# Expert weights by pairs of adjacent rows in a two-layer hybrid diffusion trunk

## The chip, the cores and the metric

The kernel runs on one core of one Trainium2 chip. The metric is the time of one execution on the device in microseconds (us). The kernel before took 2174.04, 2175.32 and 2178.39 us in three runs, median 2175.32. The profile is one execution, taken by the hardware profiler. Its engines are PE (matmul), PEld (PE's weight loads), DVE, ACT, POOL and SP; SP computes nothing and issues most of the transfers, a few are issued by ACT. Sixteen DMA engines carry all transfers.

## The reference

Two layers of one trunk run over 256 context tokens and 256 latent tokens of width 1024, all in fp32. Each layer first mixes tokens in three branches (an S5 state-space model, a Mamba-2 style SSD, windowed attention), merges them and adds the result to the stream x. Then follows the part that the change is about, a mixture of 16 experts of which each chooses its tokens. The context is routed as a set of its own, and it is not needed after layer 0, so layer 1 routes the latent tokens alone.

```python
def expert_choice_ffn(h, w_router, w_gate, w_up, w_down):
    cap = EC_CAPACITY_FACTOR * n // N_EXPERTS              # 2 * 256 / 16 = 32 tokens an expert
    aff = softmax(einsum('bnd,de->bne', h, w_router))
    g, idx = lax.top_k(swapaxes(aff, 1, 2), cap)
    xe = vmap(lambda hb, ib: hb[ib])(h, idx)                # (b, 16, 32, 1024)
    hid = silu(einsum('becd,edf->becf', xe, w_gate)) * einsum('becd,edf->becf', xe, w_up)
    ye = einsum('becf,efd->becd', hid, w_down) * g[..., None]
    # scatter-add of ye to the tokens

h2 = rmsnorm(x, norm2_g[i]) * (1.0 + sc2) + sh2             # sc2, sh2: from silu(c) @ w_mod[i] + b_mod[i]
x = x + g2 * expert_choice_ffn(h2, w_router[i], w_e_gate[i], w_e_up[i], w_e_down[i])
```

Each of the three matrices of an expert is 1024 x 1024 fp32, 4 MB; an expert has 12 MB, a layer's experts 192 MB (MB is 1,048,576 bytes where tiles are counted). In every product the sum runs over 1024 features (or 1024 hidden units), and a sum may take its terms in any order, so long as both factors use the same one.

## The kernel before, in words

**Stages.** Function `mixing` computes a layer's branches and, at its end, the router (`router_prep`, `router_half`, lines 1140 to 1200). Function `moe` (line 1239) picks the tokens (`top`, `pick`), gathers them, and goes through the 16 experts. After layer 1 a last norm writes the output. Modulation vectors (sh1, sc1, g1, sh2, sc2, g2, kinds 0 to 5) come from `mod_group` (line 159), which computes half of one vector in 32 small matmuls; these groups are filled in beside the mixing stage by `fill`. Kinds 3 and 4 are sh2 and sc2, which the experts' input uses.

**Features on partitions.** The contraction runs over partitions, so the 1024 features are cut into 8 blocks of 128. Before the change block k holds features 128k to 128k+127, partition p feature 128k + p. `gather` (line 1274) makes the transposed, selected tokens `xeT[:, k, e, :]` by a matmul of the token tile x (as weights, columns of block k) with a one-hot matrix; ScalarE or VectorE apply sc2 and sh2 per partition on the way out of PSUM. The expert's hidden units are transposed by four PE transposes (lines 1398 and 1428) into `hT`, again in blocks of 128.

**Loading the weights.** `wtiles` (line 1340) is a generator: it takes the next buffer, has SP load it, and yields the k blocks for the matmuls. A buffer of tag xw or rb8 holds 2048 columns a partition (1 MB, two blocks at full width), one of tag w, wh or wl 1024 columns (512 KB, one block). Which tag comes next is told by a list, `ring`: the first tag in it that is not larger than what is left of the matrix is taken and moved to the end. Layer 0 has 4 xw and 4 rb8, layer 1 has 6 xw and 4 rb8, both have 3 w, 2 wh and 2 wl. In layer 0 two xw buffers are lent to `s5_params`, which prepares layer 1's S5 constants during expert 4 (line 1377). The transfer itself is

```python
SP.dma_start(w, src[k0 * 128:(k0 + nk) * 128, c0:c0 + c].rearrange("(k p) c -> p k c", p=128))
```

so a partition of a large buffer receives row p of one block and row p of the next, 128 rows apart in memory: two runs of 4 KB. The down matrix of the last expert is loaded in two halves of 512 columns (`down`, line 1350), in runs of 2 KB, so that its first half can be finished early.

**Order of the work.** Gate and up take 32 matmuls an expert (line 1389 in layer 0, 1419 in layer 1), then come a tanh on ACT, two products on DVE, the transposes, and 16 matmuls of down (1405 and 1436). DVE scales the result into `YE` (1409, 1441); every four experts in layer 0 and every two in layer 1, `combine` (1363) scatters YE back to x by matmuls (1366) and adds it on DVE. Each engine's order is fixed when the program is built: a planner simulates the program and lets an instruction go ahead of others whose buffer isn't free yet in the simulation. On the chip each queue then runs strictly in that order. SP is one such queue: a transfer that waits for its buffer holds up all transfers behind it.

Of the kernel before, what the change touches and what calls it, by code (L numbers as in the profile page):

```python
# [61 lines left out]
def r(ap):  # L62
    return ap.bitcast(F32R)


@with_exitstack
def tile_trunk(ctx: ExitStack, tc: tile.TileContext, a, out, dbg=None, stop=None):
# [91 lines left out]
    def mod_group(l, kind, h):  # L159
        ps = bank("mm")  # L160
        for u in range(4):
            w = load_w(a["w_mod"][l], 2 * u, 2, kind * D + h * 512, 512, split=False)
            for i in range(2):
                for j in range(4):
                    PE.matmul(ps[32 * j:32 * j + 32, :128], sil[:, 2 * u + i, :], w[:, i, j * 128:j * 128 + 128],
                              start=u == 0 and i == 0, stop=u == 3 and i == 1)
# [296 lines left out]
    def mixing(l, mods):  # L463
# [673 lines left out]
        SP.dma_start(wr, a["w_router"][l].rearrange("(k p) e -> p k e", p=128))  # L1137
# [16 lines left out]
        def router_half(st, hf):  # L1154
            wrs, rbias = rts[st]
            xts = []
            for k2 in range(2):
                ps = bank("mm")
                for j in range(2):
                    k = 4 * hf + 2 * k2 + j  # L1160
                    for q in range(2):
                        PE.transpose(ps[:, j * 256 + q * 128:j * 256 + q * 128 + 128],
                                     x[:, 2 * st + q, k * 128:k * 128 + 128], ident)
# [75 lines left out]
    def moe(l, mods):  # L1239
# [34 lines left out]
        def gather(e0, e1, gs=sts):  # L1274
            w_ = (e1 - e0) * 32
            per = 1 if w_ * len(gs) > 512 else len(gs)
            for k in range(8):
                for s0 in range(0, len(gs), per):
                    ps = bank()
                    for si, st in enumerate(gs[s0:s0 + per]):  # L1280
                        for q in range(2):
                            tt = 2 * st + q
                            PE.matmul(ps[:, si * w_:si * w_ + w_], x[:, tt, k * 128:k * 128 + 128], oh[tt][:, e0:e1, :],  # L1283
                                      start=q == 0, stop=q == 1)
# [45 lines left out]
        def wtile(left, c):  # L1330
            tag = next(t for t in ring if (2048 if t in big else 1024) <= left * c)
# [8 lines left out]
        def wtiles(src, c0=0, c=D):  # L1340
            k0 = 0
            while k0 < 8:
                w = wtile(8 - k0, c)
                nk = w.shape[1]
                SP.dma_start(w, src[k0 * 128:(k0 + nk) * 128, c0:c0 + c].rearrange("(k p) c -> p k c", p=128))
# [29 lines left out]
        for e in range(16):  # L1375
# [8 lines left out]
            if full:  # L1384
# [12 lines left out]
                for j in range(4):  # L1397
                    PE.transpose(pt[:, j * 128:j * 128 + 128], hd[:, j * 128:j * 128 + 128], ident)
# [14 lines left out]
            else:  # L1413
# [13 lines left out]
                for j in range(4):  # L1427
                    PE.transpose(pt[:, j * 64:j * 64 + 64], hd[64:128, j * 128:j * 128 + 128], ident[64:128, 64:128])
# [75 lines left out]
def _layout(inp):  # L1504
# [8 lines left out]
    def s5cols(v):  # L1513
# [3 lines left out]

    s5d = _np.zeros((2, 8, 4, 32), g["s5_d"].dtype)
# [3 lines left out]
        "norm1": cols(g["norm1_g"]), "norm2": cols(g["norm2_g"]),  # L1522
# [5 lines left out]
        "bmod": cols(g["b_mod"]),  # L1528
# [35 lines left out]
```

## Time and profile before

| | |
|---|---|
| median of three runs | 2175.32 us (2174.04 to 2178.39) |
| profiled execution, first to last instruction | 2175.6 us |
| PE busy | 1879.4 us, 86% |
| DVE, ACT, POOL busy | 1040.2, 554.9, 589.0 us |
| moved by DMA | 561.72 MB (10^6 bytes) in 265,310 packets, mean 258 GB/s |
| share of the 16 DMA engines' time, SP's and ACT's loads | 68.0% and 3.0% |

The page cuts the span into 40 slices of 54.4 us and gives for each the busy share of each engine in tenths and the transfer rate in GB/s. The program's stages can be told in them: mixing of layer 0 to about slice 12, experts of layer 0 to slice 21, mixing of layer 1 to slice 30, then the experts of layer 1. A share of busy time is no share of what the end hangs on, since a PE that waits for data inside a run of matmuls counts as busy only in part, and matmul ends are modelled.

### The profile page before, as it was taken

How to read it: one execution, taken by the hardware profiler on the slowest of the kernel's cores; microseconds unless marked ns; L12 is line 12 of the kernel's file. 1: busy time of each engine (PE TensorE's matmuls, PEld its weight loads, DVE VectorE, ACT ScalarE, POOL GpSimd, SP SyncE). 2: the span in 40 equal slices, each digit the busy share in tenths (PEclk: the TensorE clock that was granted, in tenths of full speed). 3: DMA queues.
4: the chain of work that ended last, by engine and by line, in shares of the span. 5: the costliest groups of instructions: out<-in, count | busy, mean ns of one | idle time of the engine just before them, and what ended most of it. 6: DMA issues, size and time to landing. Idle time of an engine off the chain costs nothing. (4 is left out here: it accounts for less than half of the span.)

```text
span 2175.6 us, 29618 instructions
## 1 busy us (share of the span) xinstructions
PE 1879.4 (86%) x11292; PEld 1127.1 (52%) x11292; DVE 1040.2 (48%) x2234; ACT 554.9 (26%) x1200; POOL 589.0 (27%) x644
## 2 busy tenths in 40 slices
PE   6899999999999997986897898989998997776675
PEld 4577777788787432322332576778897322111111
DVE  6888786663256227121123469788656222212122
ACT  4335644442343100000000433535443100000000
POOL 1645476542242002000003235486533000000000
PEclk9999989999998998998898998989998899999798
DMA  9464333336345998999999355343477899999997
GB/s 268 156 183 127 114 90 107 99 104 220 90 155 203 410 349 351 409 408 409 404 409 351 107 185 172 107 129 86 125 244 271 348 409 409 409 409 409 409 409 274
DMA packets 265310, 561.72 MB, mean 258 GB/s; under 512 B 44048, under 2 KB 132560, under 8 KB 264912
## 3 DMA queue, kind: packets, MB, share of 16 engines
q1 hardware_dynamic: 232864, 541.83, 68.0%
q10 hardware_dynamic: 32304, 18.00, 3.0%
q8 instruction: 89, 1.46, 0.3%
q14 instruction: 53, 0.43, 0.1%
HBM read 552.00 MB, written 7.77 MB: 257 GB/s over the span
## 5 line engine op out<-in xcount | busy, mean ns | idle before, releaser
L122 PE MATMUL bk_mm<-hh,wh 128*128 128x512 f32 (+1 forms) x704 | 254.2, 375 | 12.5 <-ACT xp L800 6.7
L122 PE MATMUL bk_mm<-hl,wh 128*128 128x512 f32 (+1 forms) x704 | 247.6, 365 | 0.0
L113 POOL TENSOR_TENSOR wl<-w,wh 128x1024 fp32r<-128x1024 f32 x64 | 157.0, 2452 | 223.5 <-ACT wh L110 171.1
L110 ACT ACTIVATE wh<-w 128x1024 fp32r<-128x1024 f32 x140 | 147.9, 1058 | 215.9 <-PE bk_mm L122 106.6
L125 PE MATMUL bk_mm<-hh,wl 128*128 128x512 f32 (+1 forms) x704 | 163.0, 361 | 1.5 <-POOL wl L113 1.5
L122 PEld LDWEIGHTS bk_mm<-hh,wh 128*128 128x128 f32 x704 | 139.6, 199 | 36.1 <-ACT xp L800 8.2
L122 PEld LDWEIGHTS bk_mm<-hl,wh 128*128 128x128 f32 x704 | 139.6, 199 | 17.7 <-issue 1.4
L113 DVE TENSOR_TENSOR wl<-w,wh 128x1024 fp32r<-128x1024 f32 x76 | 99.8, 1315 | 72.6 <-ACT wh L110 32.4
L125 PEld LDWEIGHTS bk_mm<-hh,wl 128*128 128x128 f32 x704 | 119.6, 195 | 20.0 <-POOL wl L113 1.7
L1389 PE MATMUL bk_mm<-rb,xeT 128*64 128x512 f32 x512 | 122.1, 601 | 3.3 <-DMA rb<-w_e_up 2.0
L1419 PE MATMUL bk_mm<-xw,xeT 128*32 128x512 f32 x448 | 107.3, 628 | 16.5 <-DMA xw<-w_e_gate 11.4
L1424 DVE SCALAR_TENSOR_TENSOR hd<-fth,bk_mm 64x512 f32<-64x512 f32 x16 | 10.9, 681 | 208.4 <-ACT fth L1422 208.4
L1441 DVE SCALAR_TENSOR_TENSOR YE<-bk_mm,grow 32x512 f32<-32x512 f32 x64 | 44.0, 687 | 129.6 <-PE bk_mm L1436 115.8
L1422 ACT ACTIVATE fth<-bk_mm 64x512 f32<-64x512 f32 x16 | 9.4, 590 | 377.7 <-PE bk_mm L1419 377.7
L1389 PE MATMUL bk_mm<-xw,xeT 128*64 128x512 f32 x320 | 82.1, 613 | 13.5 <-DMA xw<-w_e_gate 13.5
L603 POOL MEMSET rb<- 128x256 f32 x2 | 1.2, 588 | 319.0 <-PE bk_mm L1389 305.0
L1393 DVE SCALAR_TENSOR_TENSOR fth<-fth,bk_mm 128x512 f32<-128x512 f32 x16 | 11.0, 687 | 157.3 <-ACT fth L1392 157.3
L1389 PEld LDWEIGHTS bk_mm<-rb,xeT 128*64 128x64 f32 x512 | 40.1, 139 | 78.6 <-issue 69.8
L1409 DVE SCALAR_TENSOR_TENSOR YE<-bk_mm,grow 32x512 f32<-32x512 f32 x64 | 44.0, 687 | 73.3 <-PE bk_mm L1405 56.5
L1419 PE MATMUL bk_mm<-rb,xeT 128*32 128x512 f32 x304 | 68.0, 603 | 8.3 <-DMA rb<-w_e_up 6.1
L1366 PE MATMUL bk_ps<-YE,Gt 128*128 128x512 f32 x128 | 61.7, 612 | 11.9 <-DVE YE L1441 9.1
L1419 PEld LDWEIGHTS bk_mm<-xw,xeT 128*32 128x32 f32 x448 | 24.1, 114 | 88.7 <-issue 55.5
(560 smaller groups left out, 3883.5 us busy)
## 6 DMA issues: line engine op xcount, KB each, us to landing
xw<-w_e_gate SPq DMA_DIRECT2D x67, 1024.0 KB, 11.5
rb<-w_e_up SPq DMA_DIRECT2D x59, 1024.0 KB, 17.4
xw<-w_e_down SPq DMA_DIRECT2D x54, 1024.0 KB, 14.0
w<-w_in SPq DMA_DIRECT2D x92, 512.0 KB, 4.7
rb<-w_e_gate SPq DMA_DIRECT2D x43, 1024.0 KB, 16.6
w<-w_mod SPq DMA_DIRECT2D x80, 512.0 KB, 4.1
xw<-w_e_up SPq DMA_DIRECT2D x29, 1024.0 KB, 14.0
w<-w_e_down SPq DMA_DIRECT2D x46, 512.0 KB, 14.0
```

Of the source, the lines that this page charges most:

```text
L110: S.activation(r(hi), raw, AF.Copy)
L113: e.tensor_tensor(r(lo), raw, hi, op=OP.subtract)
L122: PE.matmul(ps, wh(m, k), xv, start=first and k == 0 and i == 0, stop=False)
L125: PE.matmul(ps, wl(m, k), xs[k](m)[0], start=False, stop=last and k == n - 1)
L1366: PE.matmul(ps, Gt[:, tt - tts[0], e // ne, :], YE[:, tt // 2 if full else 0, n, :], start=True, stop=True)
L1389: PE.matmul(ps[64 * n:64 * n + 64, :], xeT[:, k, e, :], w[:, n * 512:n * 512 + 512], start=k == 0, stop=k == 7)
L1393: V.scalar_tensor_tensor(th, th, 1.0, pg, op0=OP.add, op1=OP.mult)
L1409: V.scalar_tensor_tensor(YE[q0:q0 + 32, si, n, :], py[o:o + 32, :], 0.5, g2[o:o + 32, si, n * 512:n * 512 + 512], op0=OP.mult, op1=OP.mult)
L1419: PE.matmul(pg[o:o + 32, :], xeT[:, k, e, :], w[:, n * 512:n * 512 + 512], start=k == 0, stop=k == 7)
L1422: S.activation(th[:64], pg[:64], AF.Tanh, scale=0.5)
L1424: V.scalar_tensor_tensor(hd[64:128], th[:64], 1.0, pg[:64], op0=OP.add, op1=OP.mult)
L1441: V.scalar_tensor_tensor(YE[q0:q0 + 32, 0, n, :], py[o:o + 32, :], 0.5, g2[o:o + 32, 1, n * 512:n * 512 + 512], op0=OP.mult, op1=OP.mult)
```

## The change

Where two neighbouring k blocks are loaded together, a partition now takes two adjacent rows, 2p and 2p + 1, of a group of 256 rows. Block k then holds features 256 (k // 2) + 2p + k % 2, which `pair(k)` names as a slice with step 2. A large buffer at full width is one run of 8 KB a partition. A large buffer is taken only where k0 is even; at an odd k0 the next small tag of the list is taken. A small buffer loads one row of each pair (runs of 4 KB, 8 KB apart). In the last expert's down matrix a large buffer of four blocks is loaded by two transfers with runs of 2 KB. Everything that meets these features takes the same order: the columns of x in the gather and in the router's transposes, the router's weights, the columns of w_mod for sh2 and sc2, the hidden units' transposes, and, on the host, norm2 and the two modulation biases.

```diff
--- before.py
+++ after.py
@@ -61,6 +61,12 @@
 
 def r(ap):
     return ap.bitcast(F32R)
+
+
+def pair(k, base=0):
+
+    o = base + (k // 2) * 256 + k % 2
+    return slice(o, o + 255, 2)
 
 
 @with_exitstack
@@ -162,7 +168,8 @@
             w = load_w(a["w_mod"][l], 2 * u, 2, kind * D + h * 512, 512, split=False)
             for i in range(2):
                 for j in range(4):
-                    PE.matmul(ps[32 * j:32 * j + 32, :128], sil[:, 2 * u + i, :], w[:, i, j * 128:j * 128 + 128],
+                    PE.matmul(ps[32 * j:32 * j + 32, :128], sil[:, 2 * u + i, :],
+                              w[:, i, pair(j) if kind in (3, 4) else slice(j * 128, j * 128 + 128)],
                               start=u == 0 and i == 0, stop=u == 3 and i == 1)
         part = small.tile([128, 128], F32, name="cpart", bufs=2)
         S.activation(part, ps[:, :128], AF.Copy)
@@ -1134,7 +1141,8 @@
         xrs = X["xrs"] = const.tile([128, 4], F32, name="xrs")
         G.memset(af, 0.0)
         wr = ep.tile([128, 8, 16], F32, name="wr")
-        SP.dma_start(wr, a["w_router"][l].rearrange("(k p) e -> p k e", p=128))
+        SP.dma_start(wr.rearrange("p (q j) e -> p q j e", j=2),
+                     a["w_router"][l].rearrange("(q p j) e -> p q j e", p=128, j=2))
         rts = {}
 
         def router_prep(st):
@@ -1160,7 +1168,7 @@
                     k = 4 * hf + 2 * k2 + j
                     for q in range(2):
                         PE.transpose(ps[:, j * 256 + q * 128:j * 256 + q * 128 + 128],
-                                     x[:, 2 * st + q, k * 128:k * 128 + 128], ident)
+                                     x[:, 2 * st + q, pair(k)], ident)
                 xt_ = ep.tile([128, 512], F32, name="xt", bufs=4)
                 if k2:
                     V.tensor_copy(xt_, ps)
@@ -1280,7 +1288,7 @@
                     for si, st in enumerate(gs[s0:s0 + per]):
                         for q in range(2):
                             tt = 2 * st + q
-                            PE.matmul(ps[:, si * w_:si * w_ + w_], x[:, tt, k * 128:k * 128 + 128], oh[tt][:, e0:e1, :],
+                            PE.matmul(ps[:, si * w_:si * w_ + w_], x[:, tt, pair(k)], oh[tt][:, e0:e1, :],
                                       start=q == 0, stop=q == 1)
                     for si, st in enumerate(gs[s0:s0 + per]):
                         so = 32 * (st - sts[0])
@@ -1327,8 +1335,9 @@
         big = {"rb8": (rb, NRB), "xw": (ap_, XW0 if full else XW)}
         ring = ["xw"] * (big["xw"][1] - 1) + RING
 
-        def wtile(left, c):
-            tag = next(t for t in ring if (2048 if t in big else 1024) <= left * c)
+        def wtile(k0, c):
+            room = (1 if c == D and k0 % 2 else 8 - k0) * c
+            tag = next(t for t in ring if (2048 if t in big else 1024) <= room)
             ring.remove(tag)
             ring.append(tag)
             if tag in big:
@@ -1340,9 +1349,18 @@
         def wtiles(src, c0=0, c=D):
             k0 = 0
             while k0 < 8:
-                w = wtile(8 - k0, c)
+                w = wtile(k0, c)
                 nk = w.shape[1]
-                SP.dma_start(w, src[k0 * 128:(k0 + nk) * 128, c0:c0 + c].rearrange("(k p) c -> p k c", p=128))
+                if nk == 1:
+                    o = (k0 // 2) * 256
+                    SP.dma_start(w, src[o:o + 256, c0:c0 + c].rearrange("(p j) c -> p j c", j=2)[:, k0 % 2:k0 % 2 + 1, :])
+                elif c == D:
+                    SP.dma_start(w.rearrange("p j c -> p (j c)"),
+                                 src[k0 * 128:(k0 + nk) * 128, :].rearrange("(p j) c -> p (j c)", j=2))
+                else:
+                    for q in range(0, nk, 2):
+                        SP.dma_start(w[:, q:q + 2, :],
+                                     src[(k0 + q) * 128:(k0 + q + 2) * 128, c0:c0 + c].rearrange("(p j) c -> p j c", j=2))
                 for j in range(nk):
                     yield k0 + j, w[:, j, :]
                 k0 += nk
@@ -1395,7 +1413,7 @@
                 V.tensor_tensor(hd, th, pu, op=OP.mult)
                 pt = bank()
                 for j in range(4):
-                    PE.transpose(pt[:, j * 128:j * 128 + 128], hd[:, j * 128:j * 128 + 128], ident)
+                    PE.transpose(pt[:, j * 128:j * 128 + 128], hd[:, pair(j)], ident)
                 hT = fp.tile([128, 2, 4, 64], F32, name="hT", bufs=2)
                 S.activation(hT.rearrange("p n j s -> p j n s"), pt.rearrange("p (j n s) -> p j n s", j=4, n=2), AF.Copy)
                 py = bank("mm")
@@ -1425,7 +1443,7 @@
                 V.tensor_tensor(hd[64:128], hd[64:128], pg[64:128], op=OP.mult)
                 pt = bank()
                 for j in range(4):
-                    PE.transpose(pt[:, j * 64:j * 64 + 64], hd[64:128, j * 128:j * 128 + 128], ident[64:128, 64:128])
+                    PE.transpose(pt[:, j * 64:j * 64 + 64], hd[64:128, pair(j)], ident[64:128, 64:128])
                 hT = fp.tile([128, 2, 4, 32], F32, name="hT", bufs=2)
                 S.activation(hT.rearrange("p n j s -> p j n s"),
                              pt[:, :256].rearrange("p (j n s) -> p j n s", j=4, n=2), AF.Copy)
@@ -1515,17 +1533,23 @@
         sl = v.reshape(2, 2, 8, 2, 2, 64).transpose(4, 5, 0, 2, 1, 3).reshape(128, 2, 32)
         return _np.concatenate([_np.concatenate([gl, gl], 0), sl], 2)
 
+    def pairs(v):
+        n = v.shape[-1] // 256
+        return _np.ascontiguousarray(v.reshape(*v.shape[:-1], n, 128, 2).swapaxes(-1, -2)).reshape(v.shape)
+
+    bmod = g["b_mod"].reshape(2, 6, 1024).copy()
+    bmod[:, 3:5] = pairs(bmod[:, 3:5])
     s5d = _np.zeros((2, 8, 4, 32), g["s5_d"].dtype)
     s5d[..., :16] = g["s5_d"].reshape(2, 8, 4, 16)
     part = {
         "c2": _np.concatenate([cols(g["c_ctx"][None]), cols(g["c"])], 1),
-        "norm1": cols(g["norm1_g"]), "norm2": cols(g["norm2_g"]),
+        "norm1": cols(g["norm1_g"]), "norm2": cols(pairs(g["norm2_g"])),
         "convw": cols(g["ssd_conv_w"]), "convb": cols(g["ssd_conv_b"]),
         "s5d": s5d.transpose(2, 3, 0, 1).reshape(128, 16),
         "bglu": cols(g["s5_b_glu"]),
         "ssdd": cols(_np.repeat(g["ssd_d"], 64, 1)), "ssdg": cols(g["ssd_norm_g"]),
         "dtb": rep(g["ssd_dt_bias"]), "alog": rep(g["ssd_a_log"]), "sink": rep(g["attn_sink"]),
-        "bmod": cols(g["b_mod"]),
+        "bmod": cols(bmod.reshape(2, 6144)),
     }
     bc = []
     for nm in ("s5_b_re", "s5_b_im", "s5_c_re", "s5_c_im"):
```

## Rows read from the trace of the kernel before

**Rows 1.** The page's 40 slices: DMA busy share in tenths, transfer rate.

```profile
DMA  9464333336345998999999355343477899999997
GB/s 268 156 183 127 114 90 107 99 104 220 90 155 203 410 349 351 409 408 409 404 409 351 107 185 172 107 129 86 125 244 271 348 409 409 409 409 409 409 409 274
```

**Rows 2.** Stretches: us, PE, PEld, DVE, ACT, POOL busy (instructions), clock, DMA share, GB/s.

```profile
864.00:1180.00 316.00, 261.46 (x1092) 85.82 (x1092) 56.40 (x85) 13.26 (x25) 5.49 (x10) 0.92 1.02 408
1701.00:2154.00 453.00, 345.43 (x1674) 95.45 (x1670) 88.58 (x132) 22.04 (x44) 0.00 (x0) 0.91 1.03 408
0.00:864.00 864.00, 799.01 (x5026) 566.42 (x5026) 530.36 (x1280) 311.12 (x675) 338.64 (x387) 0.97 0.57 187
1180.00:1701.00 521.00, 465.47 (x3478) 377.23 (x3480) 354.72 (x715) 205.59 (x449) 244.87 (x248) 0.91 0.52 161
...
109.00:544.00 435.00, 423.47 (x3049) 331.30 (x3048) 306.60 (x619) 189.59 (x444) 220.71 (x233) 0.97 0.44 131
```

**Rows 3.** The same view, short stretches of layer 0's experts.

```profile
770.00:780.00 10.00, 10.00 (x40) 4.68 (x42) 4.57 (x7) 1.26 (x3) 0.00 (x0) 1.00 0.69 262
...
850.00:860.00 10.00, 5.03 (x24) 1.44 (x20) 5.61 (x23) 0.00 (x0) 8.60 (x26) 0.93 0.55 219
860.00:870.00 10.00, 3.54 (x10) 1.21 (x12) 1.00 (x2) 0.00 (x0) 1.24 (x3) 0.50 0.73 287
...
1050.00:1060.00 10.00, 10.00 (x50) 4.11 (x48) 2.75 (x4) 0.00 (x0) 0.00 (x0) 1.00 0.99 380
```

**Rows 4.** DMA view: 1740 to 1940, 2146 to 2152, 693 to 695 us.

```profile
DMA packets 21535, 81.82 MB, mean 409 GB/s; under 512 B 1581, under 2 KB 1581, under 8 KB 21528
...
DMA packets 1178, 2.32 MB, mean 386 GB/s; under 512 B 53, under 2 KB 53, under 8 KB 1177
...
DMA packets 103, 0.84 MB, mean 422 GB/s; under 512 B 0, under 2 KB 0, under 8 KB 0
```

**Rows 5.** Chain that ended last, 1948 to 1972 us: start, us, what.

```profile
1948.23 17.99 DMA wl<-w_e_up
...
1966.27 1.95 PE bk_mm L1419 x4
...
1971.54 5.19 PE bk_mm L1436 x32
```

**Rows 6.** The page's DMA issues: KB each, median us to landing.

```profile
rb<-w_e_up SPq DMA_DIRECT2D x59, 1024.0 KB, 17.4
...
w<-w_branch SPq DMA_DIRECT2D x24, 512.0 KB, 3.7
```

**Rows 7.** SP's queue in order of time: start, us, transfer.

```profile
1943.39 4.75 SPq L1345 DMA_DIRECT2D rb<-w_e_down  x2
1948.23 2.16 SPq L1345 DMA_DIRECT2D wl<-w_e_up  x1
...
1962.50 0.33 SPq L1345 DMA_DIRECT2D wh<-w_e_gate  x1
```

**Rows 8.** Groups of instructions; last two: gather alone, by stretches.

```profile
L165 PE MATMUL bk_mm<-w,sil 128*32 128x128 f32 x1280 | 61.7, 289 | 8.1 <-DMA w<-w_mod 6.0 <-DVE mcol L181 1.8
L1283 PEld LDWEIGHTS bk_ps<-oh,x 128*128 128x128 f32 x256 | 44.3, 220 | 23.5 <-issue 10.5 <-PE bk_mm L1436 1.7 <-PE bk_mm L1405 1.6
...
682.00:762.00 80.00, 24.20 (x124) 20.20 (x124) 0.92 0.87 341
1672.00:1762.00 90.00, 22.89 (x96) 17.55 (x96) 0.84 0.93 366
```

**Rows 9.** Tile wr: its transfer's time to landing.

```profile
DMA to landing us min/median/max: 5.8/10.0/14.2
```

**Rows 10.** Order of time at the end of layer 1.

```profile
2156.01 1.98 PE L1366 MATMUL bk_ps<-YE,Gt 128*128 128x512 f32 x4 [1.49 <-DVE YE L1441]
2157.92 3.63 PE L1436 MATMUL bk_mm<-xw,hT 128*32 128x512 f32 x16
...
2158.03 0.69 DVE L1368 TENSOR_TENSOR x<-x,bk_ps 128x512 f32<-128x512 f32 x1 [0.17 <-PE bk_ps L1366]
```

## The prediction, made before the change ran

> **What bounds the kernel now.** I read the page's slices first. The reader is to see two plateaus at 409 GB/s with the DMA engines busy in nine tenths or more, slices 16 to 20 and 32 to 38, and far lower traffic everywhere else [rows 1]. The view by stretches puts numbers on them. From 864 to 1180 us (experts 5 to 15 of layer 0) and from 1701 to 2154 us (nearly all of layer 1's experts) the DMA share is 1.02 and 1.03 at 408 GB/s, while PE is busy for 261 of 316 us and for 345 of 453 us. In the other two stretches PE is busy for 799 of 864 and 465 of 521 us and the DMA engines for about half [rows 2]. So 769 us hang on transfers and 1385 us on PE and the dependences around it; the last 22 us are the tail. The chain of waits confirms it: in layer 1 it steps from a weight tile's landing to a few matmuls and back to a transfer of some 18 us [rows 5]. Those 18 us are mostly the queue: 512 KB take 3.7 us in the mixing stage, where the queue is short, and 1 MB 17.4 here [rows 6].
>
> Inside the plateaus the engines carry packets of 4 KB: from 1740 to 1940 us 81.82 MB in 21,535 packets, 1,581 of them under 512 B, so 4.1 KB for each of the others, at 409 GB/s. Two short stretches of the same trace hold other sizes. From 2146 to 2152 us the packets are rows of 2 KB (the last expert's half rows): 386 GB/s at full queues. From 693 to 695 us they are the 8 KB rows of the g2 broadcast, 103 packets, none under 8 KB: 422 GB/s [rows 4]. The rate grows with the packet, as if each cost a fixed time beside its bytes: per 4 KB on one of 16 engines 160.2 ns at 409; per 8 KB 310.6 ns at 422, 9.8 ns less than two of 4 KB.
>
> **The change part by part.** The sum is made against the profiled execution, 2175.6 us from first to last instruction, no other time is shown around it; the median of the runs is 2175.32, so a difference carries over as it is.
>
> *Expert weights.* A full-width tile of 1 MB is now 128 runs of 8 KB in place of 256 of 4 KB. Going through the ring list of the code for each matrix (a two-row tile now only at even k): layer 0 keeps 128 large and 128 small tiles, two of the large in the last down matrix with half rows, so 126 tiles get 8 KB runs; layer 1 goes from 142 large and 100 small to 140 and 104, four with half rows, so 136. The other transfers keep runs of 4 KB or 2 KB. One MB is 1.0486 MB / 409 = 2.564 us, and 2.485 us at 422: 0.079 us less. Only tiles loaded inside the two plateaus count. 316 us at 408 GB/s are 123 MB tiles' worth, the last 123 of layer 0 hold 80 such tiles: 6.3 us. 453 us are 176, the last 176 of layer 1 hold 124: 9.8 us. Together 16.1 us. Ends: 0 if the rate does not move; 20.7 us if all 262 counted. Before 864 us nothing is won: DMA waits for buffers behind PE (262 GB/s from 770 to 780), and from 850 to 870 for two xw buffers that the S5 parameters of layer 1 hold (219 and 287 GB/s) [rows 3]; a faster transfer only waits longer there. What is late next inside the plateaus is PE, with 55 of 316 and 108 of 453 us free, several times the gain.
>
> The Trainium skill says otherwise: "DMA: Bandwidth & Descriptors", section Specifications, gives 512 B as the smallest transfer that reaches line rate, by which 4 KB is there already and the kernel stays at 2175; 386, 409 and 422 GB/s [rows 4] contradict it, so far as two short stretches can.
>
> *Issues.* SP issues 506 weight transfers in place of 498, since half-row tiles of four k take two. An issue holds SP for 0.3 to 0.4 us [rows 7], 3 us in all, beside transfers that queue for 18: nothing, and 3 us if SP were empty-handed. At the very end the last matmuls start when the combine before them is through [rows 10], not on a landing: 0, between −1 and +1.
>
> *Ring order.* Since two small tiles now fill an odd place, small buffers come round sooner. Taking the oldest buffer each time, layer 0 had 4 reuses after 3 MB and 12 after 5 MB, now 16 after about 3; layer 1 had one below 6 MB, now 13 at 3. SP waits there for a matmul, and behind it on SP stand all later weights, for which PE waits. 24 of these lie in the plateaus. Value taken: 0. The nearest rows: SP's order already puts later tiles before a small one that is not free (the wl tile of 1948 us behind two down tiles), PE waits for it 18 us [rows 5, 7], and the rate holds 408. Bounds: 0, and 26 us (below).
>
> *Strided reads.* Gathers, router and hd transposes load every second column as weights; 8 of 20 modulation groups stream every second column (kinds 3 and 4). No row shows a PE read with a stride. Nearest: the same instructions at stride one, 44.3 us of gather weight loads and 61.7 us of modulation matmuls, 40% of which, 24.7, are concerned [rows 8]. I take 0. Upper end, each twice as long: 24.7 us in stretches where PE is the bound, and some 26 us of gather loads (20.2 up to 762 us and a third of 17.6 around 1701; later ones lie under saturated DMA, as hd's do). Lower end 0, a stride removes no work. The Trainium skill's "SBUF — State Buffer", section on the DMA port swizzle, says two hits in a 16-byte line keep full bandwidth, which a stride of two in fp32 just makes; no run here shows it.
>
> *Router and layout.* The router's rows go from 1024 to 512 runs. The transfer lands after 5.8 to 14.2 us [rows 9], and POOL waits for it, once per layer; its 64 KB at 409 GB/s are 0.2 us, so the rest is waiting in the queue that stays. −0.3 us, between −3 and 0. Modulation and norm vectors are permuted before the launch: 0.
>
> Sum: 2175.6 − 16.1 − 0.3 = 2159.2, so 2159.
>
> **Rivals.** *A, the rate stays at 409:* what makes 422 is not the packet but the source, since the broadcast reads one 8 KB row for all partitions, and each weight tile comes from 1 MB of memory. For it: the stretch is 2 us long. Against it: 2 KB and 4 KB rows both come from distinct addresses and already differ by 6% [rows 4]. Time 2175. The Trainium skill's rule on line rate, above, would end here too.
>
> *B, slower, the tight reuse starves the queue:* the 3 MB in between are 7.6 us of transfers; a fresh 512 KB transfer needs 3.7 us to land, 2.4 beyond its own 1.28, so PE may lag its landings by 5.2 us. After the last up tile lands at 1966.2 the first down matmul starts at 1971.5, 5.3 us later [rows 5]; a down tile that has landed in between waits about that long. So it stands at the edge. It turns the sign once a reuse loses 0.7 us, which is what the one dip inside a plateau cost, 1050 to 1060 us at 380 GB/s, 10 × (1 − 380/409) [rows 3]. At 1.1 us each, 24 reuses cost 26 us: 2185. Against it: layer 0's 12 reuses at 5 MB are already shorter than the 7 MB in flight (18 us at 0.41 MB/us), with that one dip.
>
> *C, slower, strided PE reads are slow:* at twice the time 51 us more, 2210; it decides from a third more (16/51). For it: PE is busy 0.97 of 109 to 544 us, where modulation groups are filled in [rows 2]. Against: a load of 128 fp32 columns takes PE 220 ns, 1.7 ns a column, and the modulation matmul 289 ns for 128, 2.3 ns each [rows 8]: each column already takes longer than a read of four bytes by the other engines in this trace (DVE's 512 columns in 0.69 us, 1.3 ns each [rows 10]).
>
> **How the numbers follow.** Forecast 64%, A 13%, B 14%, C 9%. The forecast's own range is 2152 to 2168: 20.7 plus 3 us of gain at one end, half the gain lost to reuse or to the planner's new order in the PE stretches at the other. The wide range goes from 2150 to 2187: it takes in A and the middle of B, and leaves out C at full price and B beyond 1.2 us a reuse. Within 0.2% is 4.4 us, about what a measurement of this kernel can tell from no change. Faster by more: 62 of the forecast's 64 points and 4 of B's and C's mild ends, 66%. Same: A's 11, the rest of the forecast and 1 of B, 13%. Slower: 21%.
>
> **What would show it.** Right: in both plateaus the rate is 417 to 418 GB/s (65% and 70% of the bytes at 422, the rest at 409); packets fall by 262 × 128 and some 1,000 router runs to about 231,000; the stretch from 1701 us to the end is some 10 us shorter, layer 0's plateau 6. A: 409 again with half the packets. B: slices of the plateaus below 400 GB/s, SP waiting for L1405, L1436 or the gate matmuls before a w, wh or wl tile. C: gather weight loads well above 220 ns, or modulation matmuls above 289 ns mean. I am wrong in the step itself if the rate rises and the time does not, which would mean that PE, not DMA, ended the plateaus.

## The result, and the profile after

The changed kernel took 2206.36 us (median of 4 runs, 2204.45 to 2207.75) against 2176.86 for the kernel before in the same comparison (4 runs, 2174.04 to 2179.96): a ratio of 1.0139, 95% interval 1.0113 to 1.0164. It is slower by about 30 us where 16 less were forecast. The profiled execution spans 2205.9 us.

First the page's slices and its packet line, which answer to [rows 1]:

```profile
DMA  9464333345257998999996453423668999999993
GB/s 269 152 191 128 98 113 90 95 139 191 87 163 265 374 377 349 416 416 416 417 417 231 146 183 116 137 63 100 184 193 302 406 394 399 417 409 410 393 416 119
DMA packets 230878, 561.72 MB, mean 255 GB/s; under 512 B 43152, under 2 KB 131664, under 8 KB 196944
```

and three stretches (us, busy times, granted clock, DMA share, GB/s), against [rows 2]:

```profile
900.00:1000.00 100.00, 80.85 (x338) 27.50 (x334) 18.53 (x27) 3.58 (x6) 0.00 (x0) 0.93 1.02 417
1000.00:1100.00 100.00, 80.10 (x328) 29.01 (x330) 17.95 (x27) 4.18 (x7) 0.00 (x0) 0.91 1.02 417
1701.00:2154.00 453.00, 339.38 (x1632) 102.10 (x1628) 87.48 (x131) 21.10 (x42) 0.00 (x0) 0.87 1.00 405
```

The packets fell to the forecast number, and layer 0's plateau runs at 416 to 417 GB/s in place of 409. Layer 1's does not: slices 31 to 38 read 406, 394, 399, 417, 409, 410, 393, 416. Where a slice is free of holes the new rate is there; the holes eat it. And the last slice carries 119 GB/s in place of 274: the weights' transfers end 42 us before the kernel does, where it was 19 in the kernel before.

Cut into stages, a profiled execution gives five lengths: to layer 0's first gather matmul (mix 0), from there to the end of its last combine matmul (experts 0), to layer 1's first gather (mix 1), to the end of its last combine matmul (experts 1), and a final norm of 10.3 to 10.5 us in all programs here. "Load" is the part of an expert stage up to its last weight landing, "tail" the rest. Each row is one execution. Two profiles of one and the same program further down (pair_l1 and pair_l1_b) differ by 4.1 us in mix 0, by 4.6 in experts 0 and mix 1 together and by 0.7 in experts 1, so differences of that size in one profile show little.

| us | mix 0 | experts 0 (load + tail) | mix 1 | experts 0 + mix 1 | experts 1 (load + tail) | span |
|---|---|---|---|---|---|---|
| before | 687.0 | 526.9 (502.3 + 24.7) | 468.4 | 995.3 | 482.7 (474.2 + 8.6) | 2175.6 |
| after | 684.5 | 517.1 (498.4 + 18.8) | 487.2 | 1004.4 | 506.6 (475.0 + 31.6) | 2205.9 |

So layer 1's experts lost 23.9 us, and the two stages ahead of them 9.1 together. The clock granted to PE does not explain the 23.9: it is 0.87 in the changed kernel's stretch above, and 0.87 as well in a stretch of the fastest kernel below (pair_l1_b, experiment 8).

Why layer 1 lost is read from single tiles. Expert 13's down matrix takes the three w buffers at blocks 0 to 2 and, by the new rule, the first of them again at block 7, after 3 MB of other tiles. SP's queue (start, us, transfer):

```profile
2083.78 2.01 SPq L1356 DMA_DIRECT2D w<-w_e_down  x3
...
2112.72 0.33 SPq L1356 DMA_DIRECT2D w<-w_e_down  x1
...
2145.55 1.86 SPq L1356 DMA_DIRECT2D w<-w_e_gate  x1
...
2153.18 0.33 SPq L1356 DMA_DIRECT2D w<-w_e_gate  x1
```

and PE in the same stretch (L1437 is gate and up, L1454 down; in brackets the idle time before and what ended it):

```profile
2110.76 2.78 PE L1454 MATMUL bk_mm<-w,hT 128*32 128x512 f32 x10 [0.53 <-ACT hT L1448]
...
2115.87 7.03 PE L1437 MATMUL bk_mm<-xw,xeT 128*32 128x512 f32 x32
2122.74 0.60 PE L1454 MATMUL bk_mm<-wl,hT 128*32 128x512 f32 x2
...
2130.57 1.03 PE L1454 MATMUL bk_mm<-w,hT 128*32 128x512 f32 x4
...
2142.58 1.03 PE L1437 MATMUL bk_mm<-wh,xeT 128*32 128x512 f32 x4
2146.78 1.92 PE L1437 MATMUL bk_mm<-wl,xeT 128*32 128x512 f32 x4 [3.17 <-DMA wl<-w_e_gate]
2158.49 1.92 PE L1437 MATMUL bk_mm<-w,xeT 128*32 128x512 f32 x4 [9.79 <-DMA w<-w_e_gate]
2163.84 1.92 PE L1437 MATMUL bk_mm<-w,xeT 128*32 128x512 f32 x4 [3.42 <-DMA w<-w_e_gate]
```

The reader is to see how long a buffer is held: block 0 is issued at 2083.78 and used from 2110.76, so block 7 cannot be issued before about 2112, 28 us after it, while 3 MB take 7.6. It goes out at 2112.72, ten places late in the queue. It is a tile of down, so PE helps itself with the next expert's gate matmuls (2115.87) and multiplies it at 2130.57. But its buffer is free only then, at 2131.6, and in expert 15 the last two small tiles of the gate matrix go out 8 and 9 places late, at 2145.55 and 2153.18. They stand so far back in the fixed order of the queue, behind tiles of up and down. There is no next expert: PE stands 9.79 and 3.42 us. The chain that ended last shows what follows:

```profile
2122.91 12.58 DMA wh<-w_e_gate
...
2135.56 17.56 DMA rb<-w_e_down
...
2153.18 10.61 DMA w<-w_e_gate
...
2163.84 11.28 PE bk_mm L1437 x52
...
2178.49 6.43 PE bk_mm L1454 x16
```

Gate and up end at 2175.1 in place of 2147.8 (6.4 us of that by the stage's later start), after the last landing at 2163.8, so down and combine stand wholly behind it. Over the stage PE's waits for small tiles of gate and up add up to 74.2 us (the first five lines; waited for: us, times, longest):

```profile
PE bk_mm L1437 <- DMA w<-w_e_gate: 30.2, 4, 15.2
PE bk_mm L1437 <- DMA wh<-w_e_up: 24.8, 2, 12.4
...
PE bk_mm L1437 <- DMA wh<-w_e_gate: 8.0, 1, 8.0
PE bk_mm L1437 <- DMA wl<-w_e_up: 8.0, 2, 4.8
...
PE bk_mm L1437 <- DMA wl<-w_e_gate: 3.2, 1, 3.2
...
PE bk_mm L1437 <- DMA xw<-w_e_up: 2.0, 2, 1.4
```

against 30.5 in the kernel before (the lines of w, wh and wl):

```profile
PE bk_mm L1419 <- DMA xw<-w_e_gate: 11.4, 11, 1.5
PE bk_mm L1419 <- DMA wl<-w_e_gate: 10.5, 3, 5.3
...
PE bk_mm L1419 <- DMA wh<-w_e_gate: 8.5, 4, 6.2
...
PE bk_mm L1419 <- DMA rb<-w_e_up: 6.1, 7, 1.5
PE bk_mm L1419 <- DMA wl<-w_e_up: 5.9, 2, 5.6
PE bk_mm L1419 <- DMA xw<-w_e_up: 5.0, 6, 1.5
PE bk_mm L1419 <- DMA wh<-w_e_up: 4.9, 3, 4.5
...
PE bk_mm L1419 <- DMA rb<-w_e_gate: 2.2, 2, 1.6
...
PE bk_mm L1419 <- DMA w<-w_e_gate: 0.7, 3, 0.2
```

Part of this only changed places: the waits for large tiles (xw, rb) fell from 24.7 us to 2.0. Both together rose from 55.2 to 76.2 us, 21.0 of the 23.9 that the stage lost.

In mix 1 one of PE's waits stands out, that for S5 constants which come back from DRAM (tile kd, 0.6 us before):

```profile
PE bk_s L720 <- DMA rb<-kd: 13.0, 3, 8.8
```

Strided reads are seen in the groups of modulation matmuls (512 of the 1,280 are strided), of gather loads and of the loads for the hidden transposes (busy us, mean ns):

```profile
L171 PE MATMUL bk_mm<-w,sil 128*32 128x128 f32 x1280 | 60.4, 290 | 11.6 <-DMA w<-w_mod 9.2 <-DVE mcol L188 2.3
L1291 PEld LDWEIGHTS bk_ps<-oh,x 128*128 128x128 f32 x256 | 46.4, 229 | 22.6 <-issue 10.1 <-PE bk_mm L1454 1.7 <-PE bk_mm L1423 1.6
...
L1416 PEld LDWEIGHTS bk_ps<-kc,fth 128*128 128x128 f32 x64 | 9.1, 207 | 22.1 <-DVE fth L1413 19.0 <-issue 2.9 <-DVE xw L311 0.2
...
L1446 PEld LDWEIGHTS bk_ps<-kc,hd 64*128 64x128 f32 x64 | 8.8, 209 | 46.7 <-DVE hd L1443 39.7 <-issue 7.0
```

The last two groups, the hidden transposes of layer 0 and of layer 1, in the kernel before:

```profile
L1398 PEld LDWEIGHTS bk_ps<-kc,fth 128*128 128x128 f32 x64 | 8.1, 160 | 24.3 <-DVE fth L1395 21.9 <-issue 2.0 <-DVE xw L304 0.2
...
L1428 PEld LDWEIGHTS bk_ps<-kc,hd 64*128 64x128 f32 x64 | 6.0, 159 | 50.5 <-DVE hd L1425 44.2 <-issue 6.3
```

### The profile page after: what moved, and what is told of

Same layout as the page of the kernel before. It is cut to its first block, busy times and chain, and to the rows that moved or that the text cites. A ratio compares the mean times of both kernels' runs of the same rounds, so it can differ in the third digit from the quotient of the medians.

```text
span 2205.9 us, 29587 instructions
## 1 busy us (share of the span) xinstructions
PE 1884.6 (85%) x11292; PEld 1144.5 (52%) x11292; DVE 1049.1 (48%) x2234; ACT 554.9 (25%) x1200; POOL 587.5 (27%) x644
## 4 chain that ended last, share of the span: by engine, by line
PE 61%; DMA 16%; DVE 14%; ACT 2%; issue 2%; POOL 2%; SPq 1%; ACTq 0%; DVEq 0%; POOLq 0%
PE bk_mm L128 12%; PE bk_mm L1437 8%; PE bk_mm L1407 8%; PE bk_mm L131 5%; DMA xw<-w_e_gate 5%; PE bk_mm L1423 4%; PE bk_mm L1454 3%; PE bk_ps L1291 3%; PE bk_ps L1384 2%; DMA w<-w_in 2%; PE bk_ps L1044 2%; DMA wh<-w_e_up 1%; PE bk_s L722 1%; DVE rb L698 1%; DMA w<-w_e_gate 1%
## 5 line engine op out<-in xcount | busy, mean ns | idle before, releaser
L1427 DVE SCALAR_TENSOR_TENSOR YE<-bk_mm,grow 32x512 f32<-32x512 f32 x64 | 44.0, 687 | 164.0 <-PE bk_mm L1423 160.2
L1437 PE MATMUL bk_mm<-xw,xeT 128*32 128x512 f32 x480 | 112.6, 652 | 2.0 <-DMA xw<-w_e_up 2.0
L1410 ACT ACTIVATE fth<-bk_mm 128x512 f32<-128x512 f32 x16 | 9.6, 597 | 256.8 <-PE bk_mm L1407 243.6
L1437 PEld LDWEIGHTS bk_mm<-xw,xeT 128*32 128x32 f32 x480 | 28.3, 121 | 83.3 <-issue 76.8
L171 PE MATMUL bk_mm<-w,sil 128*32 128x128 f32 x1280 | 60.4, 290 | 11.6 <-DMA w<-w_mod 9.2
```

The lines of the kernel that those rows point to most:

```text
L1437: PE.matmul(pg[o:o + 32, :], xeT[:, k, e, :], w[:, n * 512:n * 512 + 512], start=k == 0, stop=k == 7)
```

## The experiments

Theory R: the ring rule's 3 MB reuse costs the time. Rivals: S, the 8 KB rows or the strided reads cost it; P, the planner orders the mixing stage worse after any edit; later O and D, told with the run that they belong to. All ratios are to the kernel before, run beside; the figure is the median of all executions, the stages are those of one profiled execution. "..." in a diff stands for lines left out.

**1. The ring rule alone, in the kernel before** (ring_only).

```diff
-        def wtile(left, c):
-            tag = next(t for t in ring if (2048 if t in big else 1024) <= left * c)
+        def wtile(k0, c):
+            room = (1 if c == D and k0 % 2 else 8 - k0) * c
+            tag = next(t for t in ring if (2048 if t in big else 1024) <= room)
...
```

> The kernel before with one line of the change alone: a two-row tile goes only to an even row block, so the small buffers come round after 3 MB (13 times in layer 1, 16 in layer 0); rows stay 4 KB, features in the old order, no strided reads. Theory R (tight reuse makes small tiles late in SP's queue; PE and then DMA wait): layer 1's experts take 20 us or more longer than before (482.7 us from first gather to last combine) and the tail after the last landing is near 40 us; whole kernel 2190 to 2215, as the 8 KB rows no longer give their few us back. Rival S (the 8 KB rows or the strided reads cost the time, not the ring): 2172 to 2182, layer 1's experts within 4 us of 482.7. Rival P (any edit lets the planner order the mixing stage worse): layer 1's experts unchanged, but the stretch between the layers longer by 10 us or more: 2186 to 2196.

Measured: 2213.02 us, 1.0192 (1.0160 to 1.0223). Experts 1 511.4 (480.0 + 31.4), experts 0 + mix 1 1007.5. Its stretches:

```profile
864.00:1160.00 296.00, 245.02 (x1020) 85.07 (x1018) 49.45 (x72) 11.94 (x20) 0.00 (x0) 0.92 1.03 409
1701.00:2154.00 453.00, 335.15 (x1632) 99.00 (x1628) 87.45 (x131) 21.09 (x42) 0.00 (x0) 0.87 1.01 401
```

One line of the change, without its rows and its strides, makes the kernel slower than the whole change does. S falls. The tail, 31.4 us, is shorter than the 40 or so that R had. P's sign in mix 1 is there too (486.5), but comes beside R's loss, not in its place.

**2. The change with the old ring** (old_ring).

```diff
-            room = (1 if c == D and k0 % 2 else 8 - k0) * c
+            room = (8 - k0) * c
...
-                if nk == 1:
-                    o = (k0 // 2) * 256
-                    SP.dma_start(w, src[o:o + 256, c0:c0 + c].rearrange("(p j) c -> p j c", j=2)[:, k0 % 2:k0 % 2 + 1, :])
+                if nk == 1 or k0 % 2:
+                    for i in range(nk):
+                        o, b = (k0 + i) // 2 * 256, (k0 + i) % 2
+                        SP.dma_start(w[:, i:i + 1, :], src[o:o + 256, c0:c0 + c].rearrange("(p j) c -> p j c", j=2)[:, b:b + 1, :])
```

> The changed kernel with the ring rule of the kernel before: a two-row tile may stand at an odd row block and is then loaded as two transfers with rows of 4 KB (4 tiles of layer 0, 48 of layer 1); all others keep 8 KB. Strided reads stay. Theory R: no 3 MB reuse is left in layer 1, so its experts fall from 506.6 us to 476 to 482 and the kernel to 2160 to 2185, depending on what the mixing stage keeps of its 19 us. Rival S: layer 1's experts stay above 500 us, the kernel above 2195. Rival P: layer 1's experts 500 us or more or less, but the stretch from the last combine of layer 0 to the first gather of layer 1 stays 10 us or more above the 468.4 of before.

Measured: 2173.54 us, 0.9992 (0.9972 to 1.0012). Experts 1 482.4 (469.8 + 12.5), mix 1 468.3. Both losses go with the ring. The load is 4.4 us shorter, with 48 of layer 1's tiles still in rows of 4 KB, but the tail 3.9 us longer, so no gain is left; this run alone doesn't tell why.

**3. Small buffers in pairs** (pair_ring).

```diff
+            if c == D and k0 % 2 == 0 and ring[0] not in big and ring[1] in big:
+                room = 0
-            tag = next(t for t in ring if (2048 if t in big else 1024) <= room)
+            tag = next(t for t in ring if (2048 if t in big else 1024) <= room) if room else next(t for t in ring if t in big)
```

> The changed kernel with a ring that uses small buffers two at a time: at an even row block where only one small buffer stands ahead of a large one, the large one is taken first and the small one waits for its fellow. Reuse distances are then at least 10 MB but for one of 5, and 283 tiles (137 and 146) come in 8 KB rows in place of 262. Theory R: layer 1's experts 470 to 480 us, the tail after the last landing some 20 us, the kernel 2150 to 2175. Rival S: it has more 8 KB rows, so it is no faster than the changed kernel: 2200 or more. Rival P: layer 1's experts 470 to 480, the stretch between the layers still 10 us or more longer than before: 2165 to 2185.

Measured: 2172.78 us, 0.9997 (0.9983 to 1.0012). Experts 1 477.1 (462.8 + 14.3), at 416 to 418 GB/s in each slice of the plateau; but experts 0 + mix 1 1000.6. R holds for layer 1; in the stretch between the layers the profile has P's form, a ring of layer 0 without any 3 MB reuse lengthens it as well. The profiled execution was the longest of the ten, 8.0 us over their median, so by how much it lengthens it is less sure.

**4. Pairs in the last expert of layer 1 alone** (last_pair), otherwise the changed kernel.

```diff
+            if not full and cur[0] == 15 and c == D and k0 % 2 == 0 and ring[0] not in big and ring[1] in big:
+                room = 0
...
+            cur[0] = e
```

> The changed kernel with the pairwise ring in the last expert of layer 1 alone, so that its gate matrix takes a large buffer at block 2 where the changed kernel takes two small ones that are issued 8 and 9 places late; the 12 other 3 MB reuses of layer 1 and all of layer 0 stay. Theory R with the end as its place (in the changed kernel the stretch from the last landing to the last combine is 31.6 us against 8.6 before, since gate/up of the last expert waits for those two tiles): that stretch falls to 10 to 16 us and the kernel to 2184 to 2192. Rival D (the loss is spread evenly over the 13 reuses, as bubbles in the transfers): 2201 to 2206. Layer 0 and the stretch between the layers as in the changed kernel under both.

Measured: 2192.37 us, 1.0078 (1.0049 to 1.0108). Experts 1 490.1 (476.3 + 13.8). D falls. The tail fell by 17.8 us and the stage by 16.5, over half of the 29.5 by which the changed kernel's stage exceeds pair_ring's, and PE's two waits of 9.79 and 3.42 us are gone: so much hung on the tiles of the last expert, the two of its gate matrix first. The other 12 reuses left their mark in the load: 476.3 against 462.8.

**5. Weights in program order** (in_order).

```diff
+        def load(dst, s_):
+            with tc.issue_after(X["wd"].ins) if "wd" in X else nullcontext():
+                X["wd"] = SP.dma_start(dst, s_)
...
-                    SP.dma_start(w, src[o:o + 256, c0:c0 + c].rearrange("(p j) c -> p j c", j=2)[:, k0 % 2:k0 % 2 + 1, :])
+                    load(w, src[o:o + 256, c0:c0 + c].rearrange("(p j) c -> p j c", j=2)[:, k0 % 2:k0 % 2 + 1, :])
```

The two other transfers of `wtiles` go through `load` in the same way.

> The changed kernel, its ring kept, with the expert weights' transfers bound to program order on SP's queue: a transfer whose buffer is not free holds the queue and is no longer passed by later ones. Theory O (not the short reuse does the harm, but that later transfers are put ahead of the tile that waits, so it is issued 7 to 10 places late with some 13 to 18 us of transfers before it): with strict order a tile lands when its turn comes, the transfers already issued cover SP's wait, layer 1's experts 472 to 485 us in place of 506.6, the kernel 2165 to 2185. Theory R in its plain form (the 3 MB reuse itself starves the queue, my rival of the prediction): SP now stalls at each of them and the stage stays at 500 us or above, the kernel at 2195 or more.

Measured: 2216.36 us, 1.0189 (1.0157 to 1.0221). Experts 1 512.3 (500.8 + 11.5). SP's longest wait for a matmul is now 20.7 us, where it was 8.6 in the changed kernel; L1458 is down, L1441 gate and up (us, times, longest):

```profile
SPq L1351 <- PE bk_mm L1458: 37.7, 5, 20.7
...
SPq L1351 <- PE bk_mm L1441: 25.7, 8, 9.9
```

O falls. But this run is no clean test by itself: tied to program order, SP fetched none of layer 1's expert tiles until the last 19 us of mix 1 (first issue 1680.2 in place of 1579.3), which can lengthen the load on its own. Its fellow has the same late start (1679.8):

**6. Program order with the pairwise ring** (pair_in_order): the diffs of 3 and 5 together.

> The changed kernel with the pairwise ring in both layers and the weights' transfers in program order. Theory O: the pairwise ring alone lost some of its gain at the end of layer 1 (14.3 us from the last landing to the last combine against 8.6 before) and in odd late tiles; in order layer 1's experts take 468 to 475 us in place of 477.1, the kernel 2162 to 2174. Rival: at distances of 10 MB nothing is late any more, so order makes no difference: 477 plus or minus 3, kernel 2170 to 2181; or SP's strict waits cost more than they save: above 2181.

Measured: 2181.93 us, 1.0038 (1.0017 to 1.0059). Experts 1 482.7 (472.2 + 10.4), so O falls here too. Between the two in program order the 3 MB rule costs 512.3 − 482.7 = 29.6 us, between the two in the planner's order 506.6 − 477.1 = 29.5 (by the ratios 1.5% and 1.4% of the whole time, with layer 0's share in them). Whether the late tile holds the queue or is passed makes no difference to the sum, only to the place: 28.6 us of it lie in the load in program order, 12.2 in the load and 17.3 in the tail in the planner's. So it is the reuse that costs, not the passing.

**7. Old ring in layer 0, pairs in layer 1** (pair_l1, and the same program again as pair_l1_b). Beside the loading of experiment 2:

```diff
-            room = (1 if c == D and k0 % 2 else 8 - k0) * c
-            tag = next(t for t in ring if (2048 if t in big else 1024) <= room)
+            room = (1 if c == D and k0 % 2 and not full else 8 - k0) * c
+            if not full and c == D and k0 % 2 == 0 and ring[0] not in big and ring[1] in big:
+                room = 0
+            tag = next(t for t in ring if (2048 if t in big else 1024) <= room) if room else next(t for t in ring if t in big)
```

> The changed kernel with the ring of the kernel before in layer 0 (two-row tiles at odd places by two transfers of 4 KB rows) and the pairwise ring in layer 1. If stages add up, each as in the run that had its ring: layer 0's experts 526.6 us, the stretch between the layers 468.2, layer 1's experts 477.1: 2168 us (2164 to 2172), faster than the kernel before by 0.2 to 0.4%. If the planner's order of one stage hangs on the ring of the next (rival P), the stretch between the layers is 475 us or more and the kernel 2173 or more.

> The same program as pair_l1, run beside pair_l1_4k: 2166 (2160 to 2172), ratio to the kernel before 0.995 to 0.9995; by the rows theory 6 to 12 us below pair_l1_4k, by the ring theory within 4 us of it.

Measured: 2166.26 us, 0.9973 (0.9950 to 0.9995), and 2166.27 us, 0.9964 (0.9945 to 0.9983). Experts 1 476.8 and 476.1, experts 0 + mix 1 992.4 and 987.8. The stages add up as forecast, and this version beats both kernels, the one before by 0.3 to 0.4%.

**8. The same ring with rows of 4 KB** (pair_l1_4k): the four new lines of the last diff in the kernel before, its loading and feature order kept.

> The kernel before (rows of 4 KB, old feature order) with the pairwise ring in layer 1 alone, to part what the ring gives from what the 8 KB rows give in the fastest kernel so far (pair_l1, 2166). If the rows give it, as my forecast had it (0.079 us a tile of 1 MB, 134 tiles in layer 1's plateau, 10.6 us): layer 1's loading at 408 to 409 GB/s, its experts 480 to 488 us, the kernel 2172 to 2180. If the ring gives it: 2163 to 2169.

Measured, beside pair_l1_b: 2176.36 us, 1.0004 (0.9987 to 1.0021). Experts 1 486.7 (475.0 + 11.7). Two stretches of it:

```profile
1700.00:2130.00 430.00, 330.95 (x1590) 86.83 (x1588) 87.37 (x130) 21.02 (x42) 0.00 (x0) 0.92 1.03 409
1750.00:1950.00 200.00, 151.29 (x730) 35.91 (x730) 37.75 (x55) 6.83 (x14) 0.00 (x0) 0.91 1.03 409
```

and the same of pair_l1_b:

```profile
1700.00:2130.00 430.00, 349.69 (x1622) 93.61 (x1620) 85.59 (x127) 19.61 (x40) 0.00 (x0) 0.89 1.02 417
1750.00:1950.00 200.00, 161.28 (x752) 41.45 (x752) 38.45 (x56) 7.80 (x16) 0.00 (x0) 0.87 1.02 417
```

Not all rows of pair_l1_b are of 8 KB. From 1750 to 1950 us its packets are

```profile
DMA packets 14099, 83.50 MB, mean 417 GB/s; under 512 B 1563, under 2 KB 1563, under 8 KB 6264
```

so 7,835 of 8 KB, 77% of the bytes. The pairwise ring alone gives nothing, and the rows, with the strided reads that they need, give 10.1 us of the median. In the profiles layer 1's experts differ by 486.7 − 476.1 = 10.6 us: what 134 tiles by 0.079 us come to.

**9. The changed rule in layer 0 alone** (tight_l0), **and with the end of layer 0 as before** (tight_l0_end: the last down matrix takes large buffers for its first half, small ones for its second). Both load as experiment 2 does.

```diff
-            room = (1 if c == D and k0 % 2 else 8 - k0) * c
+            room = (1 if c == D and k0 % 2 and full else 8 - k0) * c
...
+            if full and c < D:
+                tag = next(t for t in ring if (t in big) == (c0 == 0))
...
```

The lines from `if full` on stand in the second kernel alone.

> The changed kernel with its ring rule in layer 0 alone; layer 1 has the ring of the kernel before (two-row tiles at odd places by two transfers). If the two layers' losses add up: layer 0's experts and the stretch up to layer 1's first gather together 1004 us as in the changed kernel (995 with the old ring), layer 1's experts 482: the kernel at 2180 to 2186. If the longer stretch between the layers came from layer 1's ring (whose first tiles are fetched in that stretch): together 995, the kernel at 2172 to 2176.

> The same, but the last down matrix of layer 0 takes the two large buffers for its first half and the four small ones for its second, as the kernel before does; with the changed rule it is the other way round. Theory E (the mixing stage of layer 1 is ordered by when layer 0's last small buffers come free, since its own weights go through the same w, wh and wl buffers): layer 0's experts and the stretch after them 995 to 998 us, the kernel at 2171 to 2177. Rival: the end makes no difference (1003 us or more, 2180 or more), and what the earlier 15 reuses of layer 0 shift is carried on.

Measured: 2182.23 us, 1.0036 (1.0018 to 1.0054), and 2176.70, 1.0006 (0.9988 to 1.0023). Experts 0 + mix 1 are 999.7 and 999.9 in the profiles, experts 1 477.5 and 481.4. The first kernel settles that layer 0's own ring costs time: it differs from old_ring in that ring alone, and the interval of its ratio lies wholly above old_ring's (0.9972 to 1.0012); in the profiles the stretch is 999.7 against 994.8 us. With 477.5 it missed the 482 expected for layer 1's experts, whose ring and rows are old_ring's (482.4): what lies ahead of the stage moves it by up to 5 us. On theory E the two readings disagree, the medians for it by 5.5 us, the profiled stages against it. The profiled execution of tight_l0 is the shortest of its ten, that of tight_l0_end the second longest, and the intervals of the two ratios overlap, so E stays open. The wait that had come into mix 1 is, in tight_l0,

```profile
  PE bk_s L720: 15.6, 3
```

(PE's wait for kd: us, times) and in pair_l1_b

```profile
  PE bk_s L720: 0.5, 1
```

and 4.0 in tight_l0_end, where PE waits 8.9 for a normed tile instead. In in_order, with 1008.4 us the longest stretch of all, PE does not wait for kd at all, so this wait is not the general cause. Over all runs, layer 0's old ring gives 987.8 to 995.3 us for the stretch (five profiles), any other ring 999.7 to 1008.4 (eight, two of them in program order). With each new ring of layer 0 the waits of mix 1 stand at other places; why they cost more stays open.

## Why the prediction was wrong, point by point

- *Expert weights, −16.1 us: the rate right, the sum too large.* The rate is 416 to 417 in the untroubled slices. Layer 1's term (9.8 for 124 tiles) measured 10.6 for the 134 of pair_l1_b. Layer 0's (6.3) came to 3.0 to 4.9 in single profiles (528.7 in pair_l1_4k against 525.7 and 523.8). By the medians the rows gave 10.1 us in all. Rival A falls. By the Trainium skill's "DMA: Bandwidth & Descriptors", section Specifications, 4 KB and 8 KB rows would have run alike; 409 and 417 GB/s in the pair above, at equal rings, contradict it over 430 us and no longer only over two short stretches.
- *Ring order, value taken 0: the step that failed.* Rival B had the direction, at 14%, but was priced and argued wrongly. I held the 7.6 us of 3 MB against the time from a **landing** to its use (5.3 us), and found it at the edge. The buffer is held from its **issue** on. That was in my own rows: the small up tile issued at 1948.23 [rows 7] is first used at 1966.27 [rows 5], 18.0 us later, or 7.0 MB at 0.390 MB/us, and the large down tile of 1943.39 at 1971.54, 28.2 us or 11.0 MB. Taken over the trace of before, from issue to the tile's last matmul, the 93 small tiles of layer 1's plateau were held 19.2 us in the median and 13.8 at least (5.4 MB): none could be back after 3 MB. The old ring's distances, in layer 1 mostly 13 MB, or 33 us, had room for most but not all (the longest was held 40.2 us). I also read "PE waits for it 18 us" where the row gives the time from the wl tile's issue to its landing; PE's longest wait for such a tile was 5.6 us, as the lines of waits above show, so that row was weaker evidence for 0 than I took it for. My point that layer 0's 12 reuses at 5 MB did no harm was true and did not carry over. All of layer 0's short reuses are in down matrices, where PE can go on with the next expert, and its load does not suffer (502.4 in ring_only, 502.3 before). In layer 1, 9 of 13 are in gate or up, on which the whole expert hangs. That this difference is the reason is argued; no run moved a reuse from one matrix to another.
- *The price.* 24 to 30 us for 13 reuses, by the pair of kernels compared (29.5 against pair_ring and 24.2 against old_ring with the new rows; 28.7 against the kernel before and 24.7 against pair_l1_4k with the old rows). That is 1.9 to 2.3 each in place of B's 1.1, and not evenly: 17.8 in the tail, through the last expert. I took the tail as untouched ("0, between −1 and +1"), since its last matmuls follow a combine; with the ring the gate matrix of the last expert became what is late. The dip from 1050 to 1060 us, by which I had priced a stall, is no reuse stall of the new kind: with 16 reuses at 3 MB in layer 0, ring_only runs at 409 from 1040 to 1060, the kernel before at 393.
- *Planner's new order, "half the gain lost" at most: too small.* Experts 0 + mix 1 are 9.1 us longer than before, 16.6 longer than in pair_l1_b. That layer 0's ring does it is shown, the mechanism is not.
- *Strided reads, 0: not quite nothing, but small.* Modulation matmuls take 290 ns against 289, gather loads 229 against 220 [rows 8]. The loads of the transposes are slower: 207 ns against 160 and 209 against 159 for the hidden units (64 each), 206 against 151 in the router (48), so there the stride was not free. The busy time of all these loads rises by 6.9 us; how much of that reaches the end no run shows, and much lies beside saturated DMA. Rival C, 51 us, falls: pair_l1_b, with every strided read, is 10.1 us faster than pair_l1_4k without any. *Issues, 0, and router, −0.3:* nothing in the runs is large enough to tell them.

With the ring put right and nothing else of the change taken back but 4 tiles of layer 0, pair_l1_b takes 8.5 us less than the kernel before beside it (2166.27 against 2174.73; by the interval of the ratio 4 to 12), and pair_l1 7.3 us less. That is about half of the sum's 16.4, so the sum was too large even without the ring's loss. The pairwise ring itself may take part of it: with the old rows layer 1's experts took 486.7 us with it and 482.7 without, though one profile of each does not settle 4 us. The profiled execution of pair_l1_b spans 2159.6 us, where the sum said 2159.2, but that is luck: it was the second shortest of twelve, 4.9 us under their median, and mix 0, which nobody touched, lies between 681 and 691 us in these programs.

## What to carry to other kernels

A buffer is taken from the issue of its transfer to the last read, not from the landing. Read that time from the trace of before, multiply it by the rate, and compare it with the distance, in bytes, at which a ring comes back to the same buffer; where a rule on alignment makes some buffers come round sooner, it is the shortest distance that counts, and the matrix it falls into. A change of layout that needs such a rule should be tried without it and alone: here the good and the bad half were a few lines apart.

## What the runs showed of the hardware

A long stream with 77% of its bytes in rows of 8 KB ran at 417 GB/s (pair_l1_b), one of rows of 4 KB at 409 (pair_l1_4k), at the same share of the DMA engines' time (1.02 and 1.03). With 160.2 ns for each of the stream's 4 KB packets, as at 409 GB/s, its 8 KB packets come to some 312 ns on one of 16 engines, or 420 GB/s; that is an estimate. A weight load of 128 columns at a stride of two fp32 took 229 ns in the gather against 220 at stride one, but 206 to 209 against 151 to 160 in the transposes; why the two differ was not tried.
